# Weight sums of two GLA heads by adding transfers in DRAM, and wider splits in the second layer of a hybrid decoder trunk

## The chip, the cores and the metric

The kernel runs on one core of one Trainium2 chip. The metric is device time in microseconds: the median of three executions was 1041.81 us (1040.53 to 1042.45). One further execution was profiled; it took 1040.18 us, and all views of the profile are of that one.

The core's engines are TensorE (PE in the profile, its weight loads PEld), VectorE (DVE), ScalarE (ACT), GpSimd (POOL) and SyncE (SP), which issues the transfers. Each engine runs its own instructions in order and waits on semaphores for the others.

## What is computed

Sixteen learned meta tokens are put in front of 512 tokens of width 1024; then come one layer of gated linear attention (GLA, 4 heads), one layer of differential softmax attention (8 heads), and a final RMSNorm.

```python
def gla_branch(xn, w_in, w_gate_up, b_gate, gnorm, w_out):
    proj = xn @ w_in
    q, k, v, z, g_lr = jnp.split(proj, [...], axis=-1)
    lg = jax.nn.log_sigmoid((g_lr @ w_gate_up + b_gate).astype(f32)) / GLA_TAU
    ...
    _, o_real = lax.scan(gla_chunk, S1, (chunks(q), chunks(k), chunks(v), chunks(lg)))
    ...
    o = head_rms(o.transpose(0, 2, 1, 3)).reshape(B, L, D_INNER) * gnorm.astype(f32)
    y = jax.nn.silu(z.astype(f32)) * o
    return (y.astype(xn.dtype) @ w_out)

def diff_branch(xn, w_in, lam_vecs, gnorm, w_out, rel_table, lambda_init):
    q, k, v, z = jnp.split(xn @ w_in, 4, axis=-1)
    lam = jnp.exp(jnp.sum(lv[0] * lv[1])) - jnp.exp(jnp.sum(lv[2] * lv[3])) + lambda_init
    ...
        p = jax.nn.softmax(s, axis=-1)
        a = p[:, :, 0] - lam * p[:, :, 1]
        return jnp.einsum('bhqk,bhkv->bhqv', a, vh)
    ...
    o = head_rms(o) * gnorm.astype(f32) * (1.0 - lambda_init)
    y = jax.nn.silu(z.astype(f32)) * o.reshape(B, L, D_INNER)
    return (y.astype(xn.dtype) @ w_out)
```

All of it is float32. The kernel gets float32 precision out of faster products by splitting every operand into a high and a low part.

## The kernel before

**Split.** `split` (L238, L239) makes a high part by a ScalarE copy into the fast type and a low part by a VectorE subtraction. A product is then three: high by high, high by low, low by high.

**Weights.** The class `Weights` loads a weight tile ("raw", two buffers) by SP, and makes parts of it (splits) in a fixed order as buffers for the parts come free; when all parts of a tile are made, the tile after the next is loaded. `load_blocks` (L254) fetches a unit, 1024 rows by 256 columns of the GLA input weights, in two transfers of 512 KB; its rows in memory are pieces of 512 bytes. `load_w` (L247) fetches tiles of the other weights.

**Units.** A unit of the GLA input projection is a 2 by 2 block product: four weight blocks a11, a12, a21, a22 (128 by 512 each as stored) by two halves of the input. The first units of head 0 (v, q and k) are computed plainly. The other 20 (z of head 0, and q, k, v and z, six units a head, of heads 1 to 3) use a scheme with seven block products in place of eight (class `Unit`, matmuls at L355). It needs four sums of weight blocks, which `want_unit` forms on VectorE: `sums` makes three additions (L295) and `outer` the fourth; the sums are then split like the other blocks. These additions stand in VectorE's order among the evacuations and splits of the units in progress.

**Order.** TensorE's instructions are in the order of the program (a manual schedule); the other engines are ordered by a scheduler with priorities, and what is marked `urgent` goes ahead. `Weaver` holds a queue of generators of matmuls; `W.fill(us)` puts about so many microseconds of them between the steps of a head. So the projections of the next head fill TensorE while the present head's scores (`gla_scores`), cross blocks (`gla_ready`) and blocks (`gla_blocks`) wait for the other engines. In `gla_blocks` every block's norm goes from TensorE's product to ScalarE (squares, L1056), VectorE (L457), GpSimd (the power -1/2, L458), ScalarE (scaling, L1058) and back to TensorE (transposes, L1080).

**Start.** Head 0's units are loaded in the order v, v, q, k, z, z, and then those of head 1: q, k, v, v, z, z. Between head 0's projections and its scores the program branches (L1102, L1103) on a value that tells whether the decay is too steep for the plain formula; in the runs shown it is not.

**Second layer.** `proj_full` and `proj_real` use `project` (L346) on pairs of weight parts from `split_w`, which splits a tile half by half in two steps of 128x512. A head's `diff_steps` has four stages for every block of 128 queries: scores with softmax (L1317 on), `turn` (transposes), `values` and `rows`. The softmax scales p1 by lambda over its row sum (L1335), and then forms p0 over its row sum minus that (L1336).

Of the kernel before, what the change touches and what calls it, by code (L numbers as in the profile page):

```python
# [19 lines left out]
P = 128  # L20
# [11 lines left out]
EPS = 1e-6  # L32
# [40 lines left out]
class Weaver:  # L73


    def __init__(self):
        self.queue, self.late, self.left, self.stop = deque(), [], 0.0, None

    def add(self, gen, us=0.0):
# [105 lines left out]
def trunk(ctx, tc, x, meta, g_norm, gla_w_in, gla_w_gate_up, gla_b_gate, gla_gnorm, gla_w_out,  # L185
# [64 lines left out]
    def load_blocks(w, c0):  # L250
# [5 lines left out]
        return t  # L256

    def load(key):
        return load_w(*key) if len(key) == 4 else load_blocks(*key)

# [10 lines left out]
    W = Weaver()  # L271
    ws = Weights(lambda *key: load(key), {"pair": 2, "sum": 1, "a11": 1, "a12": 1, "a22": 1})

# [11 lines left out]

    def want_unit(w, c0):
        def single(tag, b):
# [26 lines left out]
        return a11, a12, a22, s21, s43  # L314

    def want_plain(w, c0):
# [22 lines left out]
    def project(w, xs, n0, nn, banks, ks=range(KT)):  # L339

        (wh, wl), (xh, xl) = w.t, xs
        nk = wh.shape[1]
        for k in ks:
            for n, (a, b) in enumerate(((wh, xh), (wh, xl), (wl, xh))):
                for i, bank in enumerate(banks):
                    pe.matmul(bank, a[:, k, :], b[k][:, n0 + i * nn:n0 + (i + 1) * nn],  # L346
                              start=k == 0 and n == 0, stop=k == nk - 1 and n == 2)
            yield 3 * len(banks) * max(nn / 2400.0, 0.107)
        if ks[-1] == nk - 1:
# [104 lines left out]

    def rstd_of(dst, ss, n, np_=P):

        dve.tensor_scalar(dst, ss, 1.0 / n, EPS, op0=ALU.mult, op1=ALU.add)  # L457
        pool.tensor_tensor(dst, dst, mhalf[:np_, :dst.shape[1]], op=ALU.pow)  # L458
# [391 lines left out]
    def decay(k):  # L850
# [38 lines left out]
    def second_layer_setup():  # L889
# [19 lines left out]
        dve.tensor_scalar(lam, lam, LAM_INIT, None, op0=ALU.add)  # L909
        dve.tensor_scalar(dgs, dg_sb, 0.5 * (1.0 - LAM_INIT), None, op0=ALU.mult)  # L910

# [191 lines left out]
    with tc.If(steep > 0):  # L1103
# [4 lines left out]
        sp.dma_start(hT, hT_dr)  # L1108
    W.finish(first[-1])
    token_sums(5)  # L1110
    W.settle()
# [161 lines left out]
    def q_diff_proj(hd, s):  # L1273
# [4 lines left out]
        def gen():  # L1278
            s.T = bias_tile(hd)
            s.v = [T(ep, [P, 4, 256], F32R, f"v{i}") for i in range(2)]  # L1280
            s.vm = T(ep, [M3, 256], F32R, "vm")
            for m in range(2):
                def done(pp, m=m):
                    vt = T(ep, [P, L], F32, "t", bufs=3)
                    dve.tensor_tensor(h2(vt[:, ::-1]), pp, h2(rb), op=ALU.mult)

                    def post():
                        pt, pm = to_tokens(vt, RBLK, L - 32)
# [7 lines left out]
            s.k = [T(ep, [P, 2, L], F32R, f"k{i}", bufs=1) for i in range(2)]  # L1296
            for i in range(2):
                def done(pp, i=i):
                    kt = T(ep, [P, L], F32, "t", bufs=3)
# [3 lines left out]
                yield from proj_full(done)  # L1303

            def done_q(pp):
                s.q = [T(ep, [P, 2, NR], F32R, f"q{i}", bufs=1) for i in range(2)]
                split(s.q[0], s.q[1], pp)
# [4 lines left out]
    def diff_steps(hd, s, ys):  # L1312


        def scores(b):
            r = Head()
# [5 lines left out]
            for m in range(2):  # L1322
# [12 lines left out]
            dve.tensor_scalar(r.p[1], r.p[1], st[:, 5:6], None, op0=ALU.mult)  # L1335
            dve.scalar_tensor_tensor(r.p[0], r.p[0], st[:, 4:5], r.p[1], op0=ALU.mult, op1=ALU.subtract)  # L1336
            return r

        def turn(r):
            b, a = r.b, r.p[0]  # L1340
# [8 lines left out]
            split3(r.am, pm[:32, :P], 64)  # L1349

        def values(r):
            b = r.b
# [6 lines left out]
            act.activation(r.on, po, AF.Square, accum_out=r.st[:, 6:7])  # L1359
            rstd_of(r.st[:, 7:8], r.st[:, 6:7], 256)  # L1360
            act.activation(r.on, po, AF.Copy, scale=r.st[:, 7:8])

        def rows(r):
            pt = ps_tile()
# [180 lines left out]
```

## Time and profile before

| | |
|---|---|
| median of 3 runs | 1041.81 us |
| profiled execution | 1040.18 us |
| its span, first to last instruction | 1038.4 us |
| TensorE busy | 1012.7 us, 98% |
| VectorE busy | 718.8 us, 69% |
| ScalarE busy | 543.2 us, 52% |
| GpSimd busy | 38.5 us, 4% |
| moved by DMA | 84.29 MB, 81 GB/s over the span |
| granted TensorE clock | 0.995 |

The profile names a group of instructions by line, engine and operation, and by the program's names with the buffer numbers left out: `wl<-raw,wh` writes a low part from a raw tile and its high part. An idle time with `<-` is the time that the engine sat idle before the instruction, and what ended it. TensorE's busy time is made of overlapping matmuls whose ends are modelled, so small gaps don't show in it.

### The profile page before, as it was taken

The page shows a single profiled execution, that of the slowest core. Times are in us where ns is not written, and L with a number is a line of the kernel's source. Part 1 is how long each engine was busy: PE and PEld are TensorE (multiplying, and loading weights), DVE is VectorE, ACT ScalarE, POOL GpSimd, SP SyncE. Part 2 cuts the span into 40 slices and gives each one's busy share as a digit, 9 for nine tenths or more (in the row PEclk, how much of TensorE's full clock was granted, in tenths as well). Part 3 has the DMA queues.
Part 4 walks back from the last instruction along what each step waited for, and adds up shares of the span by engine and source line. Part 5 has one row for each costly group of instructions (what it writes and reads, how often), then busy time and mean ns, then how long its engine had stood idle before and what let it go on. Part 6 is the DMA issues. An engine that isn't in the chain of part 4 may idle for free.

```text
span 1038.4 us, 18321 instructions
## 1 busy us (share of the span) xinstructions
PE 1012.7 (98%) x7347; PEld 949.6 (91%) x7347; DVE 718.8 (69%) x1441; ACT 543.2 (52%) x1198; POOL 38.5 (4%) x68
## 2 busy tenths in 40 slices
PE   8998999999999999999999999999999999999997
PEld 7997999999999989899999898998989989889995
DVE  7986887778777887564566766665758548575675
ACT  6873765266536665546444555344444445454453
POOL 1000000001000100000000000000000000000001
PEclk9998999999999999999999999999999999999999
DMA  7221323141223332124222221322222322212212
GB/s 194 72 81 45 85 62 103 51 112 42 82 81 82 82 82 82 47 77 123 82 82 92 82 92 45 97 73 82 81 92 82 93 81 79 76 61 82 81 41 82
DMA packets 99324, 84.29 MB, mean 81 GB/s; under 512 B 6029, under 2 KB 88237, under 8 KB 99232
## 3 DMA queue, kind: packets, MB, share of 16 engines
q1 hardware_dynamic: 99232, 83.05, 26.8%
q8 instruction: 59, 0.97, 0.4%
q14 instruction: 33, 0.27, 0.1%
HBM read 83.64 MB, written 2.12 MB: 83 GB/s over the span
## 4 chain that ended last, share of the span: by engine, by line
PE 81%; DVE 6%; ACT 2%; issue 1%; POOL 1%; DMA 1%; POOLq 0%; SPq 0%; DVEq 0%
PE pp L346 33%; PE ps L325 8%; PE pp L325 7%; PE bx L355 7%; PE bv L355 5%; PE bx L804 4%; PE by L355 4%; PE bv L804 2%; PE by L804 2%; PE ps L1017 2%; DVE wl L239 1%; PE ps L715 1%; POOL st L458 1%; PE ps L1343 1%; PE ps L1080 1%
## 5 line engine op out<-in xcount | busy, mean ns | idle before, releaser
L346 PE MATMUL pp<-x,wh 128*128 128x264 f32 (+1 forms) x1504 | 321.7, 323 | 0.0
L346 PEld LDWEIGHTS pp<-x,wh 128*128 128x128 f32 x1504 | 226.9, 188 | 15.6
L238 ACT ACTIVATE wh<-raw 128x512 fp32r<-128x512 f32 (+1 forms) x212 | 138.1, 681 | 121.3 <-PE pp L346 52.6
L346 PE MATMUL pp<-x,wl 128*128 128x264 f32 (+1 forms) x752 | 198.2, 319 | 0.0
L239 DVE TENSOR_TENSOR wl<-raw,wh 128x512 fp32r<-128x512 f32 (+1 forms) x212 | 156.2, 757 | 43.3 <-ACT wh L238 42.5
L346 PEld LDWEIGHTS pp<-x,wl 128*128 128x128 f32 x752 | 124.3, 188 | 10.5
L458 POOL TENSOR_TENSOR st<-st,mhalf 128x1 f32<-128x1 f32 (+1 forms) x52 | 31.7, 609 | 922.5 <-DVE st L457 922.5
L1331 ACT ACTIVATE p<-p,st 128x528 f32<-128x528 f32 (+3 forms) x64 | 36.4, 569 | 49.3 <-DVE st L1330 48.9
L325 PE MATMUL pp<-wh,x 128*128 128x256 f32 x320 | 61.3, 282 | 0.0
L325 PEld LDWEIGHTS pp<-wh,x 128*128 128x128 f32 x320 | 51.0, 189 | 0.1
L355 PE MATMUL bx<-x,wh 128*128 128x264 f32 x320 | 47.8, 287 | 0.0
L355 PE MATMUL bv<-x,wh 128*128 128x264 f32 x320 | 47.6, 287 | 0.0
L325 PE MATMUL pp<-wl,x 128*128 128x256 f32 x160 | 45.1, 282 | 0.0
L355 PEld LDWEIGHTS bx<-x,wh 128*128 128x128 f32 x320 | 42.3, 188 | 0.5 <-issue 0.4
L355 PEld LDWEIGHTS bv<-x,wh 128*128 128x128 f32 x320 | 42.4, 189 | 0.2
L1328 DVE SCALAR_TENSOR_TENSOR p<-ps,qr,T 128x264 f32<-128x264 f32 (+3 forms) x80 | 36.6, 491 | 6.4 <-PE ps L325 6.2
L374 ACT ACTIVATE u<-bx 128x264 f32<-128x264 f32 x60 | 23.0, 383 | 28.7 <-PE bx L355 26.3
L239 DVE TENSOR_TENSOR aT<-ps,aT 128x512 fp32r<-128x512 f32 (+3 forms) x32 | 15.7, 489 | 31.8 <-ACT aT L238 31.6
L325 PE MATMUL ps<-k,q 128*128 128x264 f32 (+3 forms) x240 | 36.9, 294 | 0.0
L325 PEld LDWEIGHTS ps<-k,q 128*128 128x128 f32 x240 | 33.7, 189 | 0.9
L239 DVE TENSOR_TENSOR wl<-sum,wh 128x1024 fp32r<-128x1024 f32 x20 | 24.4, 1221 | 14.1 <-ACT wh L238 12.5
L325 PE MATMUL ps<-v,aT 128*128 128x256 f32 x240 | 33.9, 282 | 0.0
(401 smaller groups left out, 2200.7 us busy)
## 6 DMA issues: line engine op xcount, KB each, us to landing
raw<-in_diff_w_in_dram SPq DMA_DIRECT2D x32, 1024.0 KB, 5.6
raw<-in_gla_w_in_dram SPq DMA_DIRECT2D x48, 512.0 KB, 5.4
raw<-in_gla_w_out_dram SPq DMA_DIRECT2D x8, 1024.0 KB
raw<-in_diff_w_out_dram SPq DMA_DIRECT2D x8, 1024.0 KB
T<-bdr SPq DMA_DIRECT2D x8, 264.0 KB
out_dram<-z SPq DMA_DIRECT2D x8, 256.0 KB, 2.0
kd<-steep SPq DMA_DIRECT2D x4, 400.0 KB
t<-steep SPq DMA_DIRECT2D x4, 264.0 KB
```

Source lines behind the costliest of these rows:

```text
L238: act.activation(hi, src, AF.Copy)
L239: dve.tensor_tensor(lo, src, hi.bitcast(F32), op=ALU.subtract)
L325: pe.matmul(ps, l, r, start=first and n == 0, stop=last and n == 2, **kw)
L346: pe.matmul(bank, a[:, k, :], b[k][:, n0 + i * nn:n0 + (i + 1) * nn], start=k == 0 and n == 0, stop=k == nk - 1 and n == 2)
L355: pe.matmul(bank[:, :HT], w[p][:, k * P:(k + 1) * P], x[q][:, k, :], start=first and i == 0, stop=i == len(PASSES) - 1, skip_group_check=n ...
L374: act.activation(t, self.bx[:, :HT], AF.Copy, scale=self.sc)
L458: pool.tensor_tensor(dst, dst, mhalf[:np_, :dst.shape[1]], op=ALU.pow)
L715: pe.transpose(pt[:, b * P:(b + 1) * P], vt[:, t0:t0 + n], ident)
L804: pe.matmul(banks[i][:, :HT], h.t[p][:, k, mm * P:(mm + 1) * P], s.y[q][k][:, i * HT:(i + 1) * HT], start=n == 0, stop=n == len(PASSES) - 1)
L1017: pe.matmul(o, s.kd[:, i, kc], s.qs[:, i, t0:t0 + n], start=i == 0, stop=i == 1)
L1328: dve.scalar_tensor_tensor(p[:, c0:c1], ps[:, :c1 - c0], qr[:, b:b + 1], s.T[:, c0:c1], op0=ALU.mult, op1=ALU.add)
L1331: act.activation(p[:, :nk], p[:, :nk], AF.Exp, bias=st[:, m:m + 1], accum_out=st[:, 2 + m:3 + m])
```

## The change

It has four parts.

1. **Sums in DRAM.** For the twelve units of heads 2 and 3, `sums_in_memory` keeps five blocks of 256 KB a unit in DRAM. A step copies five pieces of the weights there (SP, DRAM to DRAM), and adds blocks of the three units before by transfers that accumulate (GpSimd's queue), four a unit. The first five steps are called by a beat of `Weaver` after the branch, one per 16 us of matmuls; each later one when the second tile of a unit is loaded. `load_sums` loads such a unit as two raw tiles: a11, the two blocks of one pair of parts, and a12; then the blocks of the other pair and a22. `want_unit` sends these units to `want_summed`, which makes the parts with no additions on VectorE.
2. **GpSimd in program order.** The manual schedule covers GpSimd too.
3. **Wider splits.** `split_w` splits a whole tile of 128x1024 at once, and `project` takes all products with high weights before those with low ones.
4. **Second layer's blocks.** The scaling of p1 by itself is gone: a = p1 times (lambda times sum0 over sum1) minus p0, that is, the negative of the old value times sum0. The sign goes into `dgs`, and the factor sum0 into the norm's epsilon, which becomes EPS times sum0 squared (a ScalarE square of one column). The projections' evacuations and the four stages are marked `urgent`.

```diff
 def spent(self, us):
+        if self.beats:
+            self.due -= us
+            if self.due <= 0:
+                self.due += self.every
+                self.beats -= 1
+                self.beat()
...
-    ctx.enter_context(tc.manual_schedule(engines={mybir.EngineType.PE}))
+    ctx.enter_context(tc.manual_schedule(engines={mybir.EngineType.PE, mybir.EngineType.Pool}))
...
+    def load_sums(w, c0, mem, n):
+
+        t = T(wp, [P, 4, 512], F32, "raw")
+        assert n == 0 or sums_ready(mem)
+        mem = summed[mem]
+        if n == 0:
+            for i, r in ((0, 0), (3, 512)):
+                sp.dma_start(t[:, i, :].rearrange("p (k c) -> p k c", k=4),
+                             w[r:r + 512, c0:c0 + P].rearrange("(k p) c -> p k c", p=P))
+            sp.dma_start(t[:, 1:3, :], mem[0:2].rearrange("j p c -> p j c"))
+        else:
+            sp.dma_start(t[:, :3, :], mem[2:5].rearrange("j p c -> p j c"))
+            next_sums()
+        return t
...
     def split_w(raw, ca):
         nk, ncol = raw.shape[1], raw.shape[2] // 2
         wh, wl = w_pair([P, nk, ncol])
-        for ks in (slice(0, nk // 2), slice(nk // 2, nk)):
-            split(wh[:, ks, :], wl[:, ks, :], raw[:, ks, ca:ca + ncol])
+        split(wh, wl, raw[:, :, ca:ca + ncol])
         return wh, wl
...
+    summed, AHEAD = {}, 5
+
+    def sums_in_memory(keys):
+        for key in keys:
+            summed[key] = None
+        n = [0]
+
+        def plus(m, a, b):
+            pool.dma_start(m[a], m[b], accum_op=ALU.add, max_dma_last_dim=4096)
+
+        def step():
+            if n[0] < len(keys):
+                w, c0 = keys[n[0]]
+                m = summed[w, c0] = T(dp, [5, P, 512], F32, "sums", bufs=AHEAD)
+                for j, (i, r) in ((0, (0, 0)), (3, (1, 0)), (4, (1, 512)), (1, (1, 0)), (2, (0, 512))):
+                    sp.dma_start(m[j].rearrange("p (k c) -> p k c", k=4),
+                                 by_name[w][r:r + 512, c0 + i * P:c0 + (i + 1) * P].rearrange("(k p) c -> p k c", p=P))
+            for late, pairs in ((1, ((3, 0), (1, 4))), (2, ((0, 1),)), (3, ((2, 0),))):
+                if 0 <= n[0] - late < len(keys):
+                    for a, b in pairs:
+                        plus(summed[keys[n[0] - late]], a, b)
+            n[0] += 1
+        return step, lambda key: n[0] > keys.index(key) + 3
+
+    def want_summed(name, c0):
+        def pair(i):
+            return Part("pair", lambda raw: block_pair(raw[:, i:i + 2, :]))
...
+        a11, s21, a12 = single("a11", 0), pair(1), single("a12", 3)
+        s43, a22 = pair(0), single("a22", 2)
+        key = (by_name[name], c0, (name, c0))
+        ws.want(key + (0, "sums"), [a11, s21, a12])
+        ws.want(key + (1, "sums"), [s43, a22])
         return a11, a12, a22, s21, s43
...
     def project(w, xs, n0, nn, banks, ks=range(KT)):
-        for k in ks:
-            for n, (a, b) in enumerate(((wh, xh), (wh, xl), (wl, xh))):
-                for i, bank in enumerate(banks):
-                    pe.matmul(bank, a[:, k, :], b[k][:, n0 + i * nn:n0 + (i + 1) * nn],
-                              start=k == 0 and n == 0, stop=k == nk - 1 and n == 2)
-            yield 3 * len(banks) * max(nn / 2400.0, 0.107)
+        todo = [(k, wh, b) for k in ks for b in (xh, xl)] + [(k, wl, xh) for k in ks]
+        for n, (k, a, b) in enumerate(todo):
+            for i, bank in enumerate(banks):
+                pe.matmul(bank, a[:, k, :], b[k][:, n0 + i * nn:n0 + (i + 1) * nn],
+                          start=n == 0 and ks[0] == 0, stop=n == len(todo) - 1 and ks[-1] == nk - 1)
+            if n % 3 == 2:
+                yield 3 * len(banks) * max(nn / 2400.0, 0.107)
...
+    next_sums, sums_ready = sums_in_memory([("gla", c) for hd in (2, 3) for c in (
+        256 * hd, 1024 + 256 * hd, 2048 + 512 * hd, 2304 + 512 * hd, 4096 + 512 * hd, 4352 + 512 * hd)])
...
     W.finish(first[-1])
+    W.beat, W.every, W.beats = next_sums, 16.0, AHEAD
     token_sums(5)
...
-            dve.reciprocal(st[:, 4:6], st[:, 2:4])
-            dve.tensor_tensor(st[:, 5:6], st[:, 5:6], lam, op=ALU.mult)
-            dve.tensor_scalar(r.p[1], r.p[1], st[:, 5:6], None, op0=ALU.mult)
-            dve.scalar_tensor_tensor(r.p[0], r.p[0], st[:, 4:5], r.p[1], op0=ALU.mult, op1=ALU.subtract)
+
+            dve.reciprocal(st[:, 5:6], st[:, 3:4])
+            dve.scalar_tensor_tensor(st[:, 5:6], st[:, 5:6], lam, st[:, 2:3], op0=ALU.mult, op1=ALU.mult)
+            dve.scalar_tensor_tensor(r.p[0], r.p[1], st[:, 5:6], r.p[0], op0=ALU.mult, op1=ALU.subtract)
+            act.activation(st[:, 4:5], st[:, 2:3], AF.Square, scale=math.sqrt(EPS))
             return r
...
-            rstd_of(r.st[:, 7:8], r.st[:, 6:7], 256)
+            rstd_of(r.st[:, 7:8], r.st[:, 6:7], 256, eps=r.st[:, 4:5])
```

More of the change, by code (lines that the diff above doesn't have):

```diff
@@ L77, in __init__ @@
         self.queue, self.late, self.left, self.stop = deque(), [], 0.0, None
+        self.beat, self.due, self.every, self.beats = None, 0.0, 0.0, 0
     def add(self, gen, us=0.0):
@@ L314, in want_unit, with single, fn @@
         return a11, a12, a22, s21, s43
+    summed, AHEAD = {}, 5
[21 more added lines that the diff above has]
+            return Part("pair", lambda raw: block_pair(raw[:, i:i + 2, :]))
+        def single(tag, b):
+            def fn(raw):
+                t = [T(wp, [P, 512], F32R, tag + part, bufs=1) for part in "hl"]
+                split(*t, raw[:, b, :])
+                return t
+            return Part(tag, fn)
+        a11, s21, a12 = single("a11", 0), pair(1), single("a12", 3)
[3 more added lines that the diff above has]
+        ws.want(key + (1, "sums"), [s43, a22])
+        return a11, a12, a22, s21, s43
     def want_plain(w, c0):
@@ L1312, in diff_steps @@
     def diff_steps(hd, s, ys):
+        @urgent
         def scores(b):
@@ L1349, in turn @@
             split3(r.am, pm[:32, :P], 64)
+        @urgent
         def values(r):
```

17 lines of the change are left out of this document (13 added, 4 removed).

## The prediction

> **What bounds the kernel now.** I read the page first: busy time and chain. Its columns are busy time, share of the span and instructions; the second line is the chain of waits by engine.
>
> ```profile
> span 1038.4 us, 18321 instructions
> PE 1012.7 (98%) x7347; PEld 949.6 (91%) x7347; DVE 718.8 (69%) x1441; ACT 543.2 (52%) x1198; POOL 38.5 (4%) x68
> PE 81%; DVE 6%; ACT 2%; issue 1%; POOL 1%; DMA 1%; POOLq 0%; SPq 0%; DVEq 0%
> q1 hardware_dynamic: 99232, 83.05, 26.8%
> ```
>
> TensorE is busy 98% of the span. The change leaves its instructions as they are in number and shape, so it can only gain what TensorE now loses in waits, and only where those waits end on VectorE or ScalarE. Where are they? The windows answer by stage: start to end, length, then busy time of each engine (PE is the second number), granted clock, DMA share, GB/s.
>
> ```profile
> 0.00:24.00 24.00, 19.40 (x127) 16.44 (x128) 18.61 (x41) 17.66 (x31) 3.43 (x11) 1.00 0.79 199
> 24.00:86.00 62.00, 55.49 (x447) 53.65 (x447) 54.81 (x89) 41.79 (x80) 0.00 (x0) 0.98 0.26 71
> 86.00:205.00 119.00, 118.29 (x908) 111.85 (x907) 90.21 (x180) 64.22 (x131) 3.25 (x5) 0.98 0.25 72
> 205.00:440.00 235.00, 230.17 (x1781) 219.99 (x1781) 177.56 (x340) 134.39 (x272) 9.81 (x14) 1.00 0.27 77
> 490.00:1000.00 510.00, 508.40 (x3547) 473.99 (x3546) 328.09 (x673) 243.12 (x575) 15.76 (x28) 1.00 0.26 81
> ```
>
> From 205 to 440 us, where heads 1 to 3 and all twelve changed units run, TensorE idles 235.00 - 230.17 = 4.83 us. In the second layer, 490 to 1000, it idles 1.60. These 6.4 us are the ceiling of what a lighter VectorE and ScalarE can give back.
>
> **What the change takes off.** Rows: busy total, mean ns.
>
> ```profile
> L239 DVE TENSOR_TENSOR wl<-raw,wh 128x512 fp32r<-128x512 f32 x184 | 122.0, 687 | 39.7 <-ACT wh L238 39.0
> L239 DVE TENSOR_TENSOR wl<-raw,wh 128x1024 fp32r<-128x1024 f32 x28 | 34.2, 1222 | 3.7 <-ACT wh L238 3.5
> L295 DVE TENSOR_TENSOR sum<-raw 128x512 f32<-128x512 f32 x20 | 13.8, 689 | 3.7 <-DMA raw<-in_gla_w_in_dram 3.5
> L1331 ACT ACTIVATION_READ_ACCUMULATOR p<-p,st 128x1 f32 x64 | 11.9, 187 | 0.0
> L1335 DVE TENSOR_SCALAR p<-p,st x32: 291/392/495, 537.6 to 1009.6; 128x528 f32<-128x528 f32 x8, 128x400 f32<-128x400 f32 x8, 128x272 f32<-128x272 f32 x8, 128x144 f32<-128x144 f32 x8
> ACT wh L238 <- PE pp L346: 52.6, 33, 4.4
> ```
>
> - Sums: 12 of 20 units lose four VectorE additions each of 0.689 us, 33.1 us in all.
> - Wider splits: 184 steps of 0.687 us become 92 of 1.222, 126.4 - 112.4 = 14.0 us of VectorE. ScalarE saves about as much. The first half of a high part is no longer ready early, but in the second layer ScalarE waits for TensorE to free the buffer (52.6 us in 33 waits, the last row), so the split is ahead of its user; `project` also takes all high parts before the low ones, which hides the longer VectorE step.
> - Softmax: 32 scalings of p at a median of 0.392 us go, 12.5 us; a one-column ScalarE step comes, which nothing in the block waits for until its norm, two steps later. ScalarE's one-column step in the same block takes 0.187 us (L1331); 32 of them are 6 us beside ScalarE's 48% idle.
> - The `urgent` marks reorder VectorE and ScalarE in the second layer, whose whole idle time is the 1.60 us.
>
> About 60 us of VectorE work goes, all beside a TensorE that loses 6.4 us there. Bounds: 0 and -6.4. I take **-4**: two thirds, since the waits in heads 1 to 3 end partly on VectorE sums and splits, partly on ScalarE, GpSimd's power and TensorE's own results.
>
> **What it adds, and where that lands.** Sixty copies of 256 KB (five for each unit, 512-byte rows gathered into a contiguous block), 48 adding transfers from GpSimd, and loads of 1.79 MB a unit instead of 1.05. The beat in the program suggests that the copies are spread over head 0. SP's order says otherwise. First before the change, from the two plain units of head 0 (`raw_551`, `raw_562`: q and k) over its two z units (`raw_730`, `raw_905`) to the branch:
>
> ```order
> L254 DMA raw_551<-in_gla_w_in_dram 128x8x128 x2
> L892 DMA tab_4615<-in_rel_bias_dram 32x8
> L254 DMA raw_562<-in_gla_w_in_dram 128x8x128 x2
> L254 DMA raw_730<-in_gla_w_in_dram 128x8x128 x2
> L254 DMA raw_905<-in_gla_w_in_dram 128x8x128 x2
> L1102 TENSOR_LOAD fi_1004
> ```
>
> Now the same place of the change, up to `raw_730`:
>
> ```order
> L261 DMA raw_551<-in_gla_w_in_dram 128x8x128 x2
> L357 DMA sums_3862<-in_gla_w_in_dram 512x1x128 x5
> L357 DMA sums_4146<-in_gla_w_in_dram 512x1x128 x5
> L357 DMA sums_4495<-in_gla_w_in_dram 512x1x128 x2
> L261 DMA raw_562<-in_gla_w_in_dram 128x8x128 x2
> L357 DMA sums_4495<-in_gla_w_in_dram 512x1x128 x3
> L963 DMA tab_4638<-in_rel_bias_dram 32x8
> L357 DMA sums_4836<-in_gla_w_in_dram 512x1x128 x5
> L357 DMA sums_5122<-in_gla_w_in_dram 512x1x128 x5
> L357 DMA sums_5440<-in_gla_w_in_dram 512x1x128
> L261 DMA raw_730<-in_gla_w_in_dram 128x8x128 x2
> ```
>
> SP is not in the manual order, the copies depend on nothing, and the scheduler lifts them: 12 stand ahead of `raw_562`, 26 ahead of `raw_730`, 39 ahead of `raw_905`. Behind the branch the rest follows, around head 1's q unit (`raw_4190`) and k unit (`raw_4193`):
>
> ```order
> L357 DMA sums_6473<-in_gla_w_in_dram 512x1x128 x4
> L261 DMA raw_4190<-in_gla_w_in_dram 128x8x128
> L1059 ISA
> L1059 DMA kd_3899<-steep_1_148_1008 128x800
> L261 DMA raw_4190<-in_gla_w_in_dram 128x8x128
> L357 DMA sums_6473<-in_gla_w_in_dram 512x1x128
> L357 DMA sums_6621<-in_gla_w_in_dram 512x1x128 x2
> L1073 ISA
> L1073 DMA t_3909<-steep_0_147_1007 128x528
> L357 DMA sums_6621<-in_gla_w_in_dram 512x1x128 x3
> L357 DMA sums_6778<-in_gla_w_in_dram 512x1x128 x5
> L261 DMA raw_4193<-in_gla_w_in_dram 128x8x128 x2
> ```
>
> So 49 copies stand ahead of `raw_4190`'s second half and all 60 ahead of `raw_4193`. All of SP's transfers go through one queue (q1, quoted above), so a load that stands behind them gets its bytes behind theirs. What matters is how soon each load is used. The timeline (start, length, then what it waited for) and two windows:
>
> ```profile
> 23.50 0.99 SPq L254 DMA_DIRECT2D raw<-in_gla_w_in_dram  x2
> DMA to landing us min/median/max: 4.1/4.4/4.6
> 56.77 0.99 SPq L254 DMA_DIRECT2D raw<-in_gla_w_in_dram  x2
> 60.89 0.63 ACT L238 ACTIVATE a11h<-raw 128x512 fp32r<-128x512 f32 x1 [2.33 <-DMA raw<-in_gla_w_in_dram]
> 64.70 1.06 ACT L238 ACTIVATE wh<-raw 128x1024 fp32r<-128x1024 f32 x1
> 66.61 0.28 PE L726 MATMUL bv<-x,wh 128*128 128x264 f32 x1
> 82.62 0.69 DVE L295 TENSOR_TENSOR sum<-raw 128x512 f32<-128x512 f32 x1
> 98.70 0.68 DVE L295 TENSOR_TENSOR sum<-raw 128x512 f32<-128x512 f32 x1
> 115.76 0.69 DVE L295 TENSOR_TENSOR sum<-raw 128x512 f32<-128x512 f32 x1
> 57.80:61.80 4.00, 4.00 (x36) 4.00 (x35) 3.06 (x6) 1.65 (x4) 0.00 (x0) 1.00 0.94 260
> 1030.00:1033.00 3.00, 1.55 (x13) 1.34 (x11) 2.42 (x6) 1.63 (x6) 0.00 (x0) 1.00 0.47 175
> ```
>
> `raw_730` has no slack even now: ScalarE already sits 2.33 us waiting for it at 60.89. Behind that wait on ScalarE stands the k unit's first split (64.70, ends 65.76), which TensorE uses at 66.61: 0.85 us later. `raw_905`, `raw_4190` and `raw_4193` are first read at 82.62, 98.70 and 115.76 by VectorE additions, which run in order too, ahead of the evacuations that TensorE's banks need.
>
> Let c be the time of one 256 KB copy in the queue. `raw_551` is issued from 23.50 to 24.49 and lands 4.4 us on, at 28.9; a whole unit load is 1.05 MB at 260 GB/s, 4.0 us. Then the bytes arrive at
> - first half of `raw_730`: 28.9 + 26c + 4.0 + 2.0 = 34.9 + 26c, against 60.89;
> - `raw_905`: 40.9 + 39c, against 82.62;
> - `raw_4190`: 44.9 + 49c, against 98.70;
> - `raw_4193`: 48.9 + 60c, against 115.76.
>
> All four break even at c between 1.00 and 1.11 us, and above it the last grows by 60 us for each us of c. The profile shows no copy within DRAM. Lower bound: the load's pace, 0.262 MB at 260 GB/s = 1.01 us; then the four come 0.3 us late or early, cost 0. The output stores move 175 GB/s at a DMA share of 0.47, so a write is no slower a leg than a read. Upper bound: both legs, one after the other, 2.02 us; then `raw_4193` is 54 us late. I take c = 1.3, nearer the load's pace because the two legs can overlap, but above it because both now go to the same memory: late by 7.8, 9.0, 9.9 and 11.1 us. Less about 1 us of slack, TensorE loses **+10** before 120 us, where it idles only 0.71 us from 86 to 205 and has no room to win it back.
>
> The Trainium skill ("DMA: Bandwidth & Descriptors", section "Latency and other measured facts") gives 207 to 214 GB/s per direction for copies between HBM tensors with 16 KiB rows. By it an estimate of c is 1.22 us, the loss 6 us and the sum about 3 us slower; no run here shows it yet, and it speaks against the change.
>
> **GpSimd** carries the power (L458) of every block's norm, and the adding transfers now stand between them. In head 1's blocks, before:
>
> ```order
> L458 TENSOR_TENSOR st_5638<-st_5638,mhalf 128x1
> L458 TENSOR_TENSOR st_5702<-st_5702,mhalf 128x1
> L458 TENSOR_TENSOR st_5785<-st_5785,mhalf 128x1
> L458 TENSOR_TENSOR st_5859<-st_5859,mhalf 128x1
> L458 TENSOR_TENSOR st_6870<-st_6870,mhalf 16x1
> ```
>
> and now:
>
> ```order
> L527 TENSOR_TENSOR st_5755<-st_5755,mhalf 128x1
> L350 DMA sums_5584<-sums_5584 64x1024 x2
> L350 DMA sums_5440<-sums_5440 64x1024
> L350 DMA sums_5122<-sums_5122 64x1024
> L527 TENSOR_TENSOR st_5842<-st_5842,mhalf 128x1
> L527 TENSOR_TENSOR st_5920<-st_5920,mhalf 128x1
> ```
>
> Four issues come between two powers. When are those due?
>
> ```profile
> 240.25 0.55 POOL L458 TENSOR_TENSOR st<-st,mhalf 128x1 f32<-128x1 f32 x1 [4.21 <-DVE st L457]
> 246.73 0.93 POOL L458 TENSOR_TENSOR st<-st,mhalf 128x1 f32<-128x1 f32 x1 [5.93 <-DVE st L457]
> 256.24 0.66 PE L1080 MATMUL ps<-ident,t 128*128 128x128 f32 x4 [0.35 <-ACT t L1058]
> ```
>
> GpSimd idles 5.93 us there, and what the four wait for (copies, earlier additions) is tens of us old. At SP's 0.5 us an issue they take 2.0 us and hide. A late power is a late ScalarE scaling (L1058), and TensorE's turn (L1080) already waits 0.35 us for one. Bounds: 0, and the rival below; I take **+1** for this, the larger loads and their two-tile buffering together, which lie under a DMA share of 0.25 to 0.27.
>
> Sum: -4 + 10 + 1 = **+7**. The profiled execution took 1040.18 us, 1.8 around its span, and stands 1.6 below the median of 1041.81: it would become 1047, the median **1049**.
>
> **Rivals.**
> - *The copies keep the load's pace* (c up to about 1.05; the beat and the lifting harm nothing). For: 512-byte packets either way, stores as fast as loads. Against: reads and writes share one memory. Then -4 and +0 to +1: about 1038; with all idle time won, 1035.4. Chance 0.28.
> - *The legs add up*, c = 1.6 to 2.02: the last load is 29 to 54 us late, 1067 to 1092. For: each packet is moved twice. Chance 0.10.
> - *GpSimd's issues are slow*: the sum is as in the first rival, but each issue of an adding transfer takes 3 us, four take 12, 6 more than GpSimd's idle 5.93, at two blocks of head 1 and in part in heads 0 and 2: +12 to +18, 1050 to 1056; it decides from 1.5 us an issue. For: TensorE's wait at L1080. Against: nothing measured here. Chance 0.07. The Trainium skill ("SBUF — State Buffer", section "SBUF: two separate sides") says that VectorE's two-port steps lock GpSimd out of writing descriptors, 620 ns becoming 3100: that is this rival.
> - *Nothing moves*: c between 1.1 and 1.15, gain and loss cancel: 1042. Chance 0.07.
>
> **How the numbers follow.** The forecast (c from 1.15 to 1.6) has 0.48. A measurement of this kernel can tell about 0.2% (2 us) from no change. Faster: most of the first rival and a little of the fourth, 0.28; same: the rest of these two, 0.07; slower: the forecast, the second and the third rival, 0.65. The forecast's own range is 1043 to 1067. To leave out no more than 2 in 10 it has to reach down into the first rival, to 1035, and up to c of about 1.6, 1067.
>
> **What would show it.** For the forecast: a copy of 256 KB at 1.15 to 1.6 us in the queue; ScalarE's wait before the first a11h grown from 2.33 us to about 10; TensorE's busy time between 24 and 120 us thinned by about 10 us; then 205 to 440 idling 1 to 3 us instead of 4.83. Wrong if DMA is not near full from 25 to 85 us, if the loads get ahead of the copies, or if that first wait stays near 2.33. For the GpSimd rival: its idle before the power gone and L1080 waiting microseconds.

## The result, and the profile after

| | before | after |
|---|---|---|
| median | 1041.44 us (1040.06 to 1042.45, 5 runs) | 1047.16 us (1046.02 to 1047.88, 5 runs) |
| span of the profiled execution | 1038.4 us | 1045.5 us |
| VectorE busy | 718.8 us | 675.9 us |
| GpSimd busy | 38.5 us | 79.3 us |
| moved by DMA | 84.29 MB | 122.03 MB |

The changed kernel is slower by 5.7 us: ratio 1.0054, 95% interval 1.0042 to 1.0065. The spans differ by 7.1 us. The page of the changed kernel, in the lines that answer to those shown of before (the last four are queues and DMA issues: KB each, median us from issue to landing):

```profile
span 1045.5 us, 18335 instructions
PE 1017.7 (97%) x7347; PEld 955.3 (91%) x7347; DVE 675.9 (65%) x1269; ACT 538.9 (52%) x1138; POOL 79.3 (8%) x116
q1 hardware_dynamic: 126688, 108.22, 34.1%
q0 software_dynamic: 3840, 12.59, 6.9%
sums<-sums POOLq DMA_DIRECT2D x48, 256.0 KB, 5.9
raw<-sums SPq DMA_DIRECT2D x12, 768.0 KB, 4.7
```

VectorE lost 43 us of work, and the kernel got slower. The windows say in which stage (columns as before: length, busy time of PE, PEld, DVE, ACT, POOL, then granted clock, DMA share, GB/s):

```profile
24.00:86.00 62.00, 55.43 (x447) 53.38 (x445) 53.36 (x85) 41.12 (x79) 1.79 (x2) 0.98 0.97 267
86.00:205.00 119.00, 116.66 (x896) 110.26 (x897) 90.26 (x178) 62.95 (x126) 18.32 (x24) 0.98 0.61 148
205.00:255.00 50.00, 49.60 (x375) 47.70 (x374) 32.02 (x54) 31.83 (x59) 5.85 (x8) 1.00 0.49 137
255.00:285.00 30.00, 25.44 (x186) 23.70 (x185) 17.91 (x39) 14.99 (x33) 11.61 (x15) 0.89 0.98 233
300.00:440.00 140.00, 138.14 (x1080) 132.87 (x1080) 88.98 (x169) 78.23 (x152) 7.31 (x11) 1.00 0.44 133
490.00:1000.00 510.00, 509.13 (x3512) 473.71 (x3511) 308.24 (x563) 242.93 (x537) 20.46 (x29) 1.00 0.26 82
```

The start has its DMA engines full (0.97, before 0.26), and TensorE hardly minds: 55.43 us busy against 55.49. One window of 30 us, 255 to 285, stands out: TensorE 25.44 us busy, the clock at 0.89, the DMA engines at 0.98. Before the change it was:

```profile
255.00:285.00 30.00, 29.65 (x240) 27.85 (x239) 21.83 (x49) 16.61 (x37) 0.47 (x1) 1.00 0.22 71
```

A sharper view can be worked out from the two traces: every kernel here has 7347 matmuls on TensorE, in the same order but for the products inside the second layer's projections. So the start of the n-th matmul, less the start of the n-th matmul of before, is what has been lost up to there. In us, by the time in the kernel before (the experiments' columns are explained below):

```
 before  after no_sums sums_only no_adds adds_early paced head3_only
   30.7    0.5     1.1       2.2     0.0        1.6   1.0        1.4
   60.9    0.5     0.9       2.0     0.0        1.5   0.8        1.2
   98.6    2.0     1.2       4.4     0.9        3.2   2.1        2.7
  177.8    2.0     1.2       4.4     0.9        4.1   4.3        2.8
  207.7    2.5     1.2       8.9     0.9       18.9   4.2        2.7
  271.1    1.3     1.5       7.6    -0.4       17.7  13.7        2.7
  278.9    9.0     1.5      15.8     0.9       18.5  14.7        2.7
  301.7   10.0     1.5      15.9     0.9       18.5  14.7        2.7
  339.0   10.0     1.5      16.0     0.9       18.5  16.8        2.7
  389.9    7.2     1.6      13.2    -1.9       15.7  17.0       -0.0
  926.7    9.5     3.8      13.2     0.3       18.0  19.3        2.3
  935.2    8.2     2.5      13.2    -0.9       16.8  18.1        1.0
 1027.5    7.3     1.5      13.2    -1.8       15.7  17.0       -0.0
```

What is there at 30.7 differs from run to run and stands before the first copy (issued at 25.08), so columns are compared from there on. Part of it is the clock granted in the first 24 us, 0.93 in this run of the changed kernel and 1.00 in that of before. Each column is a single execution: that of sums_only took 1053.54 us, the longest of its five (the others 1048.55 to 1050.06), that of adds_early 1056.19 (the others 1054.07 to 1054.54), and that of no_adds 1038.13, the shortest of its ten (median 1039.64).

Of the change: +1.4 at the start (60.9 to 98.6), where the copies stand; the copies alone, in no_adds, cost 0.9 there. Then +0.6 up to 230, +7.7 at one place, 271 to 279, and +1.0 behind it. Won are 1.3 between 230 and 260 and 2.8 between 339 and 390, 4.1 together. The second layer creeps up by some 2 us and gives about as much back in two places.

The one place, in the timeline of the changed kernel (start, length, what it waited for):

```profile
255.66 0.54 POOL L527 TENSOR_TENSOR st<-st,mhalf 128x1 f32<-128x1 f32 x1 [5.75 <-DVE st L526]
256.19 2.44 POOL L350 DMA_DIRECT2D sums<-sums  x3
261.05 0.80 POOL L350 DMA_DIRECT2D sums<-sums  x1 [2.41 <-issue]
264.83 0.37 SPq L276 DMA_DIRECT2D raw<-sums  x1
274.85 0.63 ACT L245 ACTIVATE a22h<-raw 128x512 fp32r<-128x512 f32 x1 [5.92 <-DMA raw<-sums]
275.39 0.20 ACT L400 ACTIVATE am<-t 32x16 fp32r<-32x16 f32 x1
275.62 0.17 DVE L403 TENSOR_TENSOR am<-t,am 32x16 fp32r<-32x16 f32 x1 [5.22 <-ACT am L400]
277.12 0.42 DVE L470 TENSOR_TENSOR t<-bv,u 128x264 f32<-128x264 f32 x1
277.60 0.62 PE L424 MATMUL bv<-x,wh 128*128 128x264 f32 x3 [3.45 <-DVE t L470]
279.45 1.11 PE L784 MATMUL ps<-ident,t 128*128 128x128 f32 x4 [1.11 <-DVE cm L403]
282.06 0.78 POOL L350 DMA_DIRECT2D sums<-sums  x1 [0.61 <-issue]
```

Read it from TensorE's wait at 277.60 upwards. TensorE waits for VectorE's evacuation of a bank (L470); VectorE stands behind a small step of the scores (L403); that waits for ScalarE, and ScalarE, in order, for the second tile of a unit. The tile was issued at 264.83 and landed some 10 us later, where its median is 4.7. Before the change the same split (a22h) did not wait for a load at all, and behind the wait of now the granted clock is low:

```profile
268.23 0.63 ACT L238 ACTIVATE a22h<-raw 128x512 fp32r<-128x512 f32 x1 [0.59 <-PE by L355]
275.00:285.00 10.00, 6.29 (x28) 5.32 (x29) 6.45 (x15) 7.13 (x18) 3.15 (x4) 0.68 1.01 258
```

The first row is of before, the second a window of the changed kernel. So the 7.7 us are two things. At the matmul of 279.45 the shift has grown from 1.3 to 6.3, 5.0 us of waiting. The other 2.7 come in the next 6 us without any wait, while the granted clock is 0.57 (278 to 282 us) and 0.58 (282 to 286), and 1.00 again from 286.

At 255.66 GpSimd finished head 1's last norm; from there it issued 20 adding transfers, up to 296.70, with nothing between them in its order. While the late tile was under way, 264.83 to 274.85, these transfers (queue q0) kept the 16 DMA engines busy for 61% of the time and the loads (q1) for 40%. That is 6.1 us and 4.0 us of all engines. The same load without adding transfers (no_adds below, 263.21 to 269.38) landed in 6.2 us, with 4.4 us of q1.

### The profile page after: what moved, and what is told of

Its sections match the earlier page's. It is cut to its first block, busy times and chain, and to the rows that moved or that the text cites. A ratio compares the mean times of both kernels' runs of the same rounds, so it can differ in the third digit from the quotient of the medians.

```text
span 1045.5 us, 18335 instructions
## 1 busy us (share of the span) xinstructions
PE 1017.7 (97%) x7347; PEld 955.3 (91%) x7347; DVE 675.9 (65%) x1269; ACT 538.9 (52%) x1138; POOL 79.3 (8%) x116
## 2 busy tenths in 40 slices
DMA packets 130618, 122.03 MB, mean 117 GB/s; under 512 B 8141, under 2 KB 108781, under 8 KB 130528
## 4 chain that ended last, share of the span: by engine, by line
PE 85%; DVE 3%; ACT 1%; DMA 1%; issue 1%; POOL 0%; POOLq 0%; DVEq 0%; ACTq 0%; SPq 0%
PE pp L414 34%; PE ps L393 9%; PE pp L393 8%; PE bx L424 8%; PE bv L424 5%; PE by L424 4%; PE bx L873 4%; PE bv L873 2%; PE ps L1088 2%; PE by L873 2%; PE ps L784 1%; DMA raw<-sums 1%; PE ps L1422 1%; PE ps L1447 1%; PE ps L1151 1%
## 5 line engine op out<-in xcount | busy, mean ns | idle before, releaser
L414 PE MATMUL pp<-x,wh 128*128 128x264 f32 (+1 forms) x1504 | 263.7, 324 | 0.0
L414 PEld LDWEIGHTS pp<-x,wh 128*128 128x128 f32 x1504 | 217.6, 189 | 17.4
L245 ACT ACTIVATE wh<-raw 128x1024 fp32r<-128x1024 f32 x132 | 139.3, 1056 | 106.8 <-PE pp L414 41.2
L246 DVE TENSOR_TENSOR wl<-raw,wh 128x1024 fp32r<-128x1024 f32 x132 | 161.2, 1221 | 51.2 <-ACT wh L245 31.1
L414 PE MATMUL pp<-x,wl 128*128 128x264 f32 (+1 forms) x752 | 133.3, 321 | 0.0
L414 PEld LDWEIGHTS pp<-x,wl 128*128 128x128 f32 x752 | 109.2, 189 | 8.6
L527 POOL TENSOR_TENSOR st<-st,mhalf 128x1 f32<-128x1 f32 (+1 forms) x52 | 33.9, 651 | 781.2 <-DVE st L526 781.2
L350 POOL DMA_DIRECT2D sums<-sums x48 | 38.5, 879 | 107.7 <-DMA sums<-in_gla_w_in_dram 63.7
L873 PE MATMUL bx<-y,wh 128*128 128x264 f32 x192 | 33.7, 286 | 0.5 <-DVE hT L881 0.5
```

Of the source, the lines that this page charges most:

```text
L245: act.activation(hi, src, AF.Copy)
L246: dve.tensor_tensor(lo, src, hi.bitcast(F32), op=ALU.subtract)
L350: pool.dma_start(m[a], m[b], accum_op=ALU.add, max_dma_last_dim=4096)
L873: pe.matmul(banks[i][:, :HT], h.t[p][:, k, mm * P:(mm + 1) * P], s.y[q][k][:, i * HT:(i + 1) * HT], start=n == 0, stop=n == len(PASSES) - 1)
```

## The experiments

Each ratio is against runs of before on the same chip, with its 95% interval. Each edit is against the changed kernel, and `...` stands for lines left out.

**no_sums**: the changed kernel with `want_unit` never sent to `want_summed`.

```diff
-        if ("gla", c0) in summed:
-            return want_summed("gla", c0)
...
-    next_sums, sums_ready = sums_in_memory([...])
-    W.beat, W.every, W.beats = next_sums, 16.0, AHEAD
```

> All units are formed on VectorE again, as before the change; GpSimd in program order, the wider splits and the second layer's new blocks stay. Theory: the loss is made by the sums in DRAM (about +2 us by the copies at the start, +7.7 us by one late tile load near 270 us, and 2 to 3 us won back in heads 2 and 3 by the lighter VectorE), and the other parts move little: 1040 to 1043 us, no stall near 270 us, TensorE's shift against before under 1 us at 440 us. Rival: the wider splits, GpSimd's program order or the second layer's blocks cost something themselves: 1044 us or more.

Measured: 1040.9 us, 0.9991 (0.998 to 1.0001). The stall near 270 us is gone. The shift at 440 us is 1.8, of which 1.1 stands there at 30.7 already. The other parts together are not told from no change: they lose 2.2 us slowly from 390 to 927 and win 1.3 at 927 and 1.0 near 1020.

**sums_only**: the complement, with narrow splits, the old order of products and the old second layer.

```diff
-        split(wh, wl, raw[:, :, ca:ca + ncol])
+        for ks in (slice(0, nk // 2), slice(nk // 2, nk)):
+            split(wh[:, ks, :], wl[:, ks, :], raw[:, ks, ca:ca + ncol])
...
```

> Only the sums in DRAM and GpSimd's program order; narrow splits and the second layer as before the change. Theory: the same 1046 to 1049 us as the whole change, with the same late tile load near 270 us. Rival (other parts carry the loss): 1044 us or less.

Measured: 1049.39 us, 1.0071 (1.0057 to 1.0085), 0.4 above the range expected. The late tile is there again, with ScalarE waiting 6.64 us for it:

```profile
281.85 0.63 ACT L245 ACTIVATE a22h<-raw 128x512 fp32r<-128x512 f32 x1 [6.64 <-DMA raw<-sums]
188.12 0.63 ACT L245 ACTIVATE a11h<-raw 128x512 fp32r<-128x512 f32 x1 [3.18 <-DMA raw<-in_gla_w_in_dram]
```

A second load, at 188.12, is late as well (+4.5 between 177.8 and 207.7, where the change has 0.5). This trace is of the execution of 1053.54 us, 3.5 to 5 us longer than the other four, so the second stall may not be in them. By the medians the whole loss is in the sums. The gains of 1.3 and 2.8 us are in this column too, so they come from the sums as well, and not from the wider splits.

**adds_early**: all steps by the beat.

```diff
-    W.beat, W.every, W.beats = next_sums, 16.0, AHEAD
+    W.beat, W.every, W.beats = next_sums, 8.0, 15
-    summed, AHEAD = {}, 5
+    summed, AHEAD = {}, 15
```

> All fifteen steps come from the beat, one per 8 us, so that the 48 adding transfers are issued in head 0 and early in head 1, before head 2's first tiles are loaded; nothing else differs. Theory (the late load near 270 us shares the DMA engines with a burst of adding transfers): no ScalarE wait of 5.9 us for raw from the sums, DMA share under 0.6 from 255 to 285 us, and 1039 to 1042 us, 5 to 8 less than the change. Rival (a unit in two tiles with two buffers leaves the second tile too little time in any case): the wait stays near 5 us and the time at 1045 to 1048 us. Second rival: the burst moves to 140 to 210 us and makes head 1's loads late there: the shift of TensorE grows by 3 us or more before 205 us.

Measured: 1054.32 us, 1.0119 (1.0104 to 1.0135). The time forecast was wrong, the second rival right: the burst moved, and the stall with it. Near 270 only 0.8 us are left; from 139 to 212 us, where 34 adding transfers now stand, the DMA engines are at 0.94, and TensorE loses some 15 us there (the x36 of GpSimd in the first row are these and two powers).

```profile
139.00:212.00 73.00, 69.30 (x526) 65.64 (x525) 48.70 (x97) 31.10 (x63) 28.04 (x36) 0.95 0.94 188
255.00:285.00 30.00, 30.00 (x224) 28.55 (x224) 22.03 (x41) 16.96 (x32) 2.03 (x3) 1.00 0.33 105
189.67 0.63 ACT L245 ACTIVATE a11h<-raw 128x512 fp32r<-128x512 f32 x1 [4.99 <-DMA raw<-in_gla_w_in_dram]
```

That is strong evidence for the burst: same transfers, same two-tile loads, another place, and the stall goes where they go.

**sp_order**: SyncE in program order too.

```diff
-engines={mybir.EngineType.PE, mybir.EngineType.Pool}
+engines={mybir.EngineType.PE, mybir.EngineType.Pool, mybir.EngineType.SP}
```

> SyncE is put in program order too, so that the copies stand where the beat and the loads call them, not at the start. Theory: the start's +2 us is gone (TensorE's shift at 125 us under 0.8 us instead of 2.0), but seven units' copies now come beside the loads of heads 1 and 2 and the adding transfers wait for them, so the load near 270 us is no earlier: 1043 to 1050 us in all. Rival (the start's loss is not the copies): shift of 2 us at 125 us as in the change.

Measured: 1072.91 us, 1.0295 (1.0281 to 1.0309), 23 us beyond the upper end expected. At the start the theory held: with no copies there (DMA share 0.26 from 24 to 86) the matmuls from 30.7 to 98.6 lose nothing (the shift goes from 2.5 to 1.9), so the loss at the start does come with the copies. The rest was not foreseen: in program order head 1's first loads stand behind other transfers and waits (TensorE waits 5.34 us for a11h at 123.18), and the copies now stand beside the loads up to 352 us. Another 7.5 us go between 490 and 550, where no copy stands; their cause stays open.

**no_adds**: the adding transfers left out.

```diff
-            pool.dma_start(m[a], m[b], accum_op=ALU.add, max_dma_last_dim=4096)
+            pass
```

> The 48 adding transfers are left out, so that the blocks in DRAM stay plain copies and the sums of heads 2 and 3 are missing from the result; copies, two-tile loads of 1.79 MB a unit and GpSimd's order stay. Theory (the adding transfers alone make the tile near 270 us late): no wait of ScalarE for raw from the sums above 1 us, TensorE's shift against before stays under 3 us from 125 to 300 us and falls by about 4 us in heads 2 and 3: 1037 to 1040 us. Rival (the larger loads in two tiles with two buffers are late by themselves): the stall of several us near 270 us stays, 1043 us or more.

Measured: 1039.64 us, 0.9978 (0.9968 to 0.9987): 2.5 us less than before, some 8 less than the change, but without the sums in its result. All of the gain of 4.1 us is there (1.3 and 2.8), the copies cost 0.9, and at 271 to 279 the loss is 1.3 instead of 7.7:

```profile
255.00:285.00 30.00, 28.92 (x234) 27.06 (x233) 21.01 (x45) 16.18 (x36) 0.00 (x0) 1.00 0.32 109
ACT a22h L245 <- DMA raw<-sums: 2.8, 2, 2.2
```

The second row, of the waits from 205 to 440 us, is total, times and longest: 2.2 us where the change has 5.9. So the rival has a small part of the truth. A second tile that can only be loaded when the tile before it is free is late by itself, for 1.3 us; the adding transfers make 6.4 of the 7.7, the low clock behind the stall included (here it stays at 1.00).

**paced**: a step's adding transfers wait until the tile loaded before has landed.

```diff
+            if 0 < n[0] < len(keys) + 3:
+                pool.tensor_copy(seen, raw[0:1, 0, 0:1])
...
         if n == 0:
+            next_sums(before)
...
-            next_sums()
-    W.beat, W.every, W.beats = next_sums, 16.0, AHEAD
```

> A step's adding transfers are issued only after GpSimd has read one number of the tile that was loaded before, and the steps come at the loads of head 1's units and of the first tile of each later unit, so that no more than one step of four stands ahead of a load; all 48 are done. Theory (it is the burst that makes loads late): the stall near 270 us shrinks from 7.7 us to under 2, no stall over 1 us at w_out's loads near 185 us, 1037 to 1042 us. Rival 1 (GpSimd's waits for tiles hold up the norms' powers behind them): TensorE waits microseconds for ps at the blocks of heads 0 to 2, 1044 us or more. Rival 2 (48 transfers of this kind are too much for the DMA engines wherever they stand): waits of 2 us or more for several loads from 130 to 300 us, 1044 us or more.

Measured: 1057.71 us, 1.0151 (1.0135 to 1.0168). The loss near 270 shrank to 1.0, as wanted, but rival 1 cost more. A norm's power now stands in GpSimd's order behind a wait for a tile and a wait for an earlier addition:

```profile
238.43 0.17 POOL L361 COPY seen<-raw 1x1 f32<-1x1 f32 x1 [3.30 <-DMA raw<-sums]
246.35 0.80 POOL L357 DMA_DIRECT2D sums<-sums  x1 [4.99 <-issue]
246.89 0.86 POOL L536 TENSOR_TENSOR st<-st,mhalf 128x1 f32<-128x1 f32 x1
247.78 0.69 ACT L1138 ACTIVATE t<-ps,st 128x512 f32<-128x512 f32 x1 [5.98 <-POOL st L536]
248.53 1.12 PE L1160 MATMUL ps<-ident,t 128*128 128x128 f32 x4 [7.41 <-ACT t L1138]
```

The chain can be read row by row: GpSimd, ScalarE's scaling, TensorE's transposes. In the changed kernel ScalarE's waits for a power from 205 to 440 us are 1.6 us at most. The smaller losses of this column, 2.2 us from 98.6 to 177.8 and 2.1 from 301.7 to 339.0, are not explained, so the second rival is not excluded.

**head3_only**: half as many sums.

```diff
-    sums_in_memory([("gla", c) for hd in (2, 3) for c in (
+    sums_in_memory([("gla", c) for hd in (3,) for c in (
```

> Only head 3's six units get their sums in DRAM (30 copies, 24 adding transfers); head 2's units are loaded and summed as before the change. Theory: only some 8 adding transfers instead of 25 follow head 1's last norm, and the tiles that are loaded beside them are whole units two ahead of use, so the stall near 270 us is gone; the gain in heads 2 and 3 shrinks from about 4 us to the 2.8 of the stretch from 335 to 390 us; the start still loses about 1 us: 1038 to 1041 us. Rival (any burst of such transfers makes a load late): a stall of 2 us or more between 130 and 300 us, 1042 us or more.

Measured: 1039.85 us, 0.9986 (0.9977 to 0.9995), as the theory had it: no step in the column from 98.6 to 339.0, 2.7 won from 339 to 390, 1.5 lost at the start. Behind head 1's last norm GpSimd issues 8 adding transfers here; in the changed kernel the trace has 20, not 25.

**gpsimd_adds**: no sums in DRAM; GpSimd adds on the raw tiles.

```diff
         def add(o, a, b):
-            dve.tensor_tensor(o, a, b, op=ALU.add)
+            pool.tensor_tensor(o, a, b, op=ALU.add)
...
```

> No sums in DRAM at all; the four additions of each of the 20 units are made by GpSimd on the raw tiles instead of VectorE, in the scheduler's order; wider splits and the second layer's new blocks stay. No trace here shows such an addition on GpSimd; VectorE takes 0.689 us. If it takes 2 us or less and holds nobody up, four fit beside a unit and VectorE's 55 us of additions cost TensorE nothing: the 4 us gain without copies and adding transfers, 1036 to 1039 us. Rival (an addition takes over 3 us, or slows VectorE's steps beside it, or the norms' powers wait behind additions): sums late at many units, 1044 us or more.

Measured: 1064.87 us, 1.0221 (1.0202 to 1.0239). The rival, though an addition takes only 1.4 to 1.6 us. Rows of GpSimd (busy, mean ns), and a moment of GpSimd and VectorE:

```profile
L318 POOL TENSOR_TENSOR raw<-raw 128x512 f32<-128x512 f32 x20 | 32.7, 1637 | 0.0
154.95 0.55 POOL L525 TENSOR_TENSOR st<-st,mhalf 128x1 f32<-128x1 f32 x1
156.27 0.66 PE L1147 MATMUL ps<-ident,t 128*128 128x128 f32 x4 [2.51 <-ACT t L1125]
147.92 1.29 POOL L318 TENSOR_TENSOR raw<-raw,sum 128x512 f32<-128x512 f32 x1 [2.11 <-DVE a12l L246]
148.09 2.20 DVE L246 TENSOR_TENSOR wl<-sum,wh 128x1024 fp32r<-128x1024 f32 x1 [0.31 <-ACT wh L245]
```

The power at 154.95 stands behind three additions, and TensorE waits 2.51 us for it. And VectorE's split beside an addition takes 2.20 us instead of 1.22.

**head3_held**: as head3_only, with the copies of a unit held back by a write of GpSimd's.

```diff
                 m = summed[w, c0] = T(dp, [5, P, 512], F32, "sums", bufs=AHEAD)
+                pool.dma_start(m[:, 0, 0:1], ident[0:5, 0:1])
...
```

> As head3_only, but GpSimd first writes one number into each of a unit's five blocks in its program's order, and the copies of the unit wait for that write, so that SyncE can't issue them at the start. Theory (the copies at the start make the first z unit's tile late): TensorE's shift against before grows by less than 0.4 us from 30 to 95 us instead of 1.4, the gain of 2.7 us in head 3 stays: 1037 to 1039.5 us. Rival (the copies, now behind the branch and in front of head 1's first units in SyncE's order, make those late): a stall of 2 us or more between 95 and 200 us, 1041 us or more.

Measured: 1046.53 us, 1.0047 (1.0034 to 1.0061). From 30.7 to 98.6 the matmuls lost nothing (2.0 to 1.6), so the start's loss comes with the copies once more; and the rival came true. In SyncE's order the load of an output weight now stands behind thirteen copies, which themselves wait for GpSimd's writes (12.4 us from 140 to 166):

```profile
143.88 20.03 SPq L358 DMA_DIRECT2D sums<-in_gla_w_in_dram  x13
164.02 0.56 SPq L254 DMA_DIRECT2D raw<-in_gla_w_out_dram  x1
176.44 1.06 ACT L245 ACTIVATE wh<-raw 128x1024 fp32r<-128x1024 f32 x1 [5.67 <-DMA raw<-in_gla_w_out_dram]
179.29 1.06 PE L1089 MATMUL ps<-qs,kd 128*32 128x128 f32 x4 [5.49 <-DVE kd L1093]
```

**head3_old_order**: as head3_only, `project` as before the change.

```diff
-        todo = [(k, wh, b) for k in ks for b in (xh, xl)] + [(k, wl, xh) for k in ks]
+        for k in ks:
+            for n, (a, b) in enumerate(((wh, xh), (wh, xl), (wl, xh))):
...
```

> As head3_only, but each chunk of the second layer's projections takes its three products together again (high by high, high by low, low by high); the splits stay wide. If the new order of products is what makes TensorE's shift creep up by 1.9 us from 440 to 925 us, the creep falls under 0.6 us and the time to 1038 to 1039.5 us. Rival (the order was needed, because a wide low part comes later): stalls at the start of weight pairs, 1041 us or more. If the creep stays, its cause is elsewhere (the blocks of the second layer): 1039 to 1041 us.

Measured: 1038.8 us, 0.9977 (0.9968 to 0.9986). The creep from 445.8 to 926.7 fell from 2.0 us (head3_only) to 0.8, not quite under 0.6, and no stall came in its place. This version beats both kernels, by 2.5 us and by some 8.

**no_sums_old_order**: the same without any sums in DRAM.

> As no_sums, with the products of the second layer's projections in the old order: no sums in DRAM at all, wider splits and the second layer's new blocks. The difference to head3_old_order is head 3's sums alone. By the traces they win 2.7 us in head 3 and cost 1.4 at the start: 1039.5 to 1041 us, about 1.3 more than head3_old_order. Rival (head 3's sums are worth nothing net): 1038.5 to 1039.3 us.

Measured: 1040.13 us, 0.9989 (0.998 to 0.9998). That is 1.3 us more than head3_old_order, the size that the traces give for head 3's sums, but the two intervals overlap.

## Why the prediction was right, and where it was not

The forecast was 1049 us, and 1047.16 came: size and sign were right, but two terms of the sum, -4 + 10 + 1, were wrong and made up for each other. That the total fits is luck.

- **-4, the lighter VectorE: right.** The shift gives 4.1 us, in heads 1 to 3 where the prediction put it, and no_adds shows the same 4.1 without the loss beside it. The share of two thirds was a guess, though, and the parts were not told apart: the sums alone bring the 4.1 (sums_only), while the second layer, with the wider splits and the new blocks, gives nothing net. In it the new order of products costs about 1 us by itself (head3_old_order). VectorE's busy time fell by 43 us and not by about 60: the rows' lengths add up to 56 us less, and busy time counts overlapping steps once.
- **+10, the copies: the step that failed is "I take c = 1.3".** The place was right: the copies stand where the order said, the DMA engines are full, and ScalarE's first a11h waits 3.74 us instead of 2.33. The price was not. The issue queue shows it in the changed kernel:

```profile
58.40 12.60 SPq L357 DMA_DIRECT2D sums<-in_gla_w_in_dram  x13
47.30 8.86 SPq L357 DMA_DIRECT2D sums<-in_gla_w_in_dram  x11
62.84 0.63 ACT L245 ACTIVATE a11h<-raw 128x512 fp32r<-128x512 f32 x1 [3.74 <-DMA raw<-in_gla_w_in_dram]
```

  Thirteen in 12.60 us and eleven in 8.86: 0.97 and 0.81 us a copy with the queue full, below even the lower bound of 1.01. The bytes say the same: 297 and 305 GB/s moved in these two stretches, 0.88 and 0.86 us for 256 KB. So a copy costs no more here than a load of its size. The loss at the start is 1.4 us, not 10, and the formula has no term for it: with c of 0.81 to 0.97 it lands `raw_730` at 56.0 to 60.1, in time. The load was issued at 57.32, 0.55 us later than before, which is the shift that the run already had. Up to ScalarE's read it took 5.5 us instead of 4.1, with copies still in flight. The sign that the prediction named against itself, a first wait that stays near 2.33, came close to true. The first rival, copies at the load's pace, was right about them, yet not about the time.
- **+1, GpSimd, larger loads and two-tile buffering: mis-sized, it measured 9.3** (0.6 + 7.7 + 1.0; the 7.7 with 2.7 of low clock). The failed sentence is that these "lie under a DMA share of 0.25 to 0.27". That is the share before the change and an average. By the page, 48 adding transfers take 6.9% of 16 engines over 1045.5 us, 1.5 us of all engines each, and GpSimd, which waits for nobody but the norms and earlier additions, issues 20 in a row behind head 1's last norm. A unit's loads are also a little larger than the prediction has them: seven blocks of 0.262 MB, 1.84 MB and not 1.79.
- **The rival of slow issues: refuted.** An issue takes 0.79 us, not 3, and four of them between two norms did hide. But they took 5.2 us, not 2.0, with a gap of 1.91 us in front of the fourth, and left 0.78 us to spare:

```profile
243.02 2.47 POOL L350 DMA_DIRECT2D sums<-sums  x3
247.40 0.79 POOL L350 DMA_DIRECT2D sums<-sums  x1 [1.91 <-issue]
248.97 0.93 POOL L527 TENSOR_TENSOR st<-st,mhalf 128x1 f32<-128x1 f32 x1 [0.78 <-DVE st L526]
```

  GpSimd was the right engine to doubt, but for what its transfers do to others' loads, not for its own lateness. The prediction looked at the four issues between two powers and not at the gap after a head's last power, where the order puts no limit.

What stays open: why the changed kernel's burst from 139 to 180 us costs 0.5 us and the same in sums_only 4.5. That the loads there have just enough slack in the one and not in the other is a guess; since the sums_only trace is of its longest execution, it may also be that execution alone. Open too is what made the 0.6 us by which the start loses more in the change than in no_adds.

## What to carry to other kernels

Work moved to DMA is not free because the DMA share is low on average: work out how long all of it takes, and ask what paces it. An otherwise idle engine, working in order, issues one transfer after the other up to its next wait for another engine, and the loads that happen to fall into that burst pay. A dose that fits the slack (half the sums, here) can win where the whole loses; pacing by waits on an engine that others also wait for costs more than the burst.

## What the hardware showed that was not expected

- Copies from DRAM to DRAM in rows of 512 bytes ran at 0.81 to 0.97 us per 256 KB with the queue full, 270 to 324 GB/s by the issues and 297 to 305 by the bytes moved, no slower than loads (260 GB/s in the prediction's window). The Trainium skill ("DMA: Bandwidth & Descriptors", section "Latency and other measured facts") gives at best 207 to 214 GB/s per direction for copies between HBM tensors; for this pattern the measurement is higher.
- An adding transfer costs the DMA engines more than a copy of the same size: 1.5 us of all 16 against some 0.8. The first is q0's 6.9%; the second is q1's growth of 78 us of all engines for 25.17 MB more, copies and larger loads together.
- Behind a stall of TensorE the granted clock fell to about half for some microseconds: 0.57 and 0.58 from 278 to 286 us in the changed kernel. After the wait of 1.08 us at the same place in no_adds it stayed at 1.00.
- VectorE's split with two SBUF inputs took 2.20 us instead of 1.22 beside a GpSimd addition that ended 1.1 us into it, nearly as if it had begun anew when that was over. The Trainium skill ("SBUF — State Buffer", section "SBUF: two separate sides") says that such a step and a GpSimd step that reads SBUF lock each other out for the whole instruction: this row agrees. The same section of the Trainium skill has a transfer issued from GpSimd go from 620 to 3100 ns beside a two-port step of VectorE, because the descriptors wait. No issue here shows such a wait: the 48 took 778 to 1401 ns. No run shows whether any of them stood beside such a step.
